# Attention slots of a one-core hybrid decoder block: query loads and splits earlier, the next head's keys and values split during its predecessor's fourth query block, reciprocals beside the first transposes

## The chip, the cores and the metric

The kernel runs on one core of one Trainium2 chip. The metric is the device time of one execution in microseconds (us); lower is better. Before the change it takes 2336.98 us as the median of three runs (2335.45 to 2340.22). The engines are called PE (matrix multiplies and transposes), ACT (activations and copies), DVE and POOL (elementwise work), and SP, which only issues the DMAs of this kernel. Each engine works through its own instructions in the order in which the program lists them; an instruction that waits holds up everything behind it on that engine.

## The reference, cut to what matters

One decoder block on 2048 positions of width 1024: a projection, eight heads of causal "forgetting" attention beside a gated linear recurrence, an output projection, and a gate with a second embedding. Only the attention is touched here. Per head of width 128, with `c` the running sum of the log forget gates:

```
s = einsum('bhqd,bhkd->bhqk', qi, k) * scale
s = s + (ci[:, :, :, None] - c[:, :, None, :])
s = where(kpos[None, :] <= qpos[:, None], s, -inf)
w = softmax(s, axis=-1)
o = einsum('bhqk,bhkd->bhqd', w, v)
```

Everything is float32. The kernel gets there with three matrix multiplies for every product: each operand is split into a rounded high part and the remainder, `hi` and `lo`, and hi·hi, hi·lo and lo·hi are added up (`mm3`).

## The kernel before, in words

The program has three parts: the projections and the recurrence, which spill queries, keys, values and gates to DRAM; the attention; and the output projections.

The attention is written as a list of **slots** that run one after the other, in an order fixed by hand. A head has 40 of them. They belong to four query blocks `g` of 512 queries: block 0 attends to 512 keys and owns slots 0 to 3, block 1 slots 4 to 11, block 2 slots 12 to 23, block 3 slots 24 to 39. A (head, block) pair is a stage, `n` in the code, and `t0[n]` is its first slot. One slot handles one piece of 128 keys (`sb`). In the order of the code, slot `t` does the following (`run_slot`, L800):

- the loads registered under `before` (SP);
- the score pieces that fall due (`score_units`, L612): three matmuls on PE from `qh`, `ql`, `kh`, `kl` into one of four score banks (`sbank`), then on DVE one custom instruction that adds the bias or the masked diagonal `dg` and keeps the running minimum `m` of the negated scores (L625, followed by a short read of `m`). These are the scores of the *next* stage: those of block `g` are spread over the slots of the block ahead of it, beginning three slots before its `t0` (LEAD). So block 1's start at slot 37 of the head before, block 2's at slot 1, block 3's at slot 9, and the next head's block 0's at slot 21;
- `add_values` (L670) for slot `t-3`: three matmuls on PE from `th`, `tl` and `vh`, `vl` into the single output bank `obank`. After a stage's last one, `finish_unit` (L686) multiplies `obank` with the spread reciprocals `rb` on DVE, which frees the bank; the next stage's first `add_values` waits for it;
- `turn_probs` (L658): PE transposes four blocks of probabilities into `tbank` (L663), ACT copies them to `th`, DVE takes the remainder `tl`;
- `spread_sums` (L678), in a stage's second slot: PE transposes the reciprocals `r4` (L682), ACT copies them to `rb`;
- on DVE the gating `gs` (L691) of a finished stage; on ACT the exponentials of complete score rows (L634), and behind the fourth of them on DVE the reciprocal of the four row sums (L638);
- what is registered under `after`: the splits. `split_u` (L509) splits the queries, the high part `qh` on ACT and the rest `ql` on DVE, and adds the causal mask to the four `dg` on POOL (L516). `split_piece` (L468) splits one of the eight pieces of the next head's keys and values, `kh`/`vh` on ACT and `kl`/`vl` on POOL. `add_squares` (L693) runs on POOL two slots after a finished stage.

Where the splits fall is set by a few numbers. For stage `n`, `s0` is the slot of its first score piece; its queries, bias and diagonals are loaded at `lo`, and split and masked at `min(lo+4, s0-1)`. That is slot 33 for the next head's block 1, slot 0 for block 2, slot 5 for block 3, slot 17 for the next head's block 0. Key and value pieces 0 to 7 of the next head are split at slots 6, 10, 14 and so on to 34, each loaded six slots earlier into one of three `kvf` buffers. The query load has one buffer, `qf`. All loads and the store of `gs` go through SP in the order of the code.

## Time and profile before

One execution was profiled. Its own time is 2336.76 us, its span 2335.0 us from the first to the last instruction.

| | us |
|---|---|
| median of three runs | 2336.98 |
| the profiled execution | 2336.76 |
| its span | 2335.0 |
| attention: first score matmul to last gating | 1138.4 to 1745.1 |
| one head in the middle (third head: slot 0's transposes to the fourth head's) | 1295.43 to 1367.02 |
| granted PE clock, mean | 0.996 |

All times below are from the start of the span. In the timeline a row has a start, a duration, the engine, the line, what is written from what, a count, and in brackets the idle time of the engine just before it with what ended it. Consecutive instructions of an engine overlap a little in the records, so the distance between two starts, not the duration, is what one costs in a queue: a `tl` of 0.69 us is followed 0.60 us later. The rows of the third head stand for all of them, since the heads repeat.

### The profile page before, as it was taken

How to read it: one execution, taken by the hardware profiler on the slowest of the kernel's cores; microseconds unless marked ns; L12 is line 12 of the kernel's file. 1: busy time of each engine (PE TensorE's matmuls, PEld its weight loads, DVE VectorE, ACT ScalarE, POOL GpSimd, SP SyncE). 2: the span in 40 equal slices, each digit the busy share in tenths (PEclk: the TensorE clock that was granted, in tenths of full speed). 3: DMA queues.
4: the chain of work that ended last, by engine and by line, in shares of the span. 5: the costliest groups of instructions: out<-in, count | busy, mean ns of one | idle time of the engine just before them, and what ended most of it. 6: DMA issues, size and time to landing. Idle time of an engine off the chain costs nothing.

```text
span 2335.0 us, 30636 instructions
## 1 busy us (share of the span) xinstructions
PE 2272.2 (97%) x11425; PEld 1890.0 (81%) x11425; DVE 1215.0 (52%) x2190; ACT 931.8 (40%) x1558; POOL 670.6 (29%) x597
## 2 busy tenths in 40 slices
PE   8999999999999999999899999999999999999999
PEld 8998888888888888888777777787878787888887
DVE  5222675454545454545577787777833213333333
ACT  7311443333333333332466666666644323221211
POOL 0220332323232323223133334343444223322221
PEclk9999999999999999999999999999999999999999
DMA  9411111111212121212444455445435435433332
GB/s 335 136 51 37 52 63 62 55 65 51 70 50 70 50 71 47 71 46 95 156 113 132 140 153 134 120 131 133 146 113 191 164 120 194 127 109 117 109 108 80
DMA packets 169012, 249.02 MB, mean 107 GB/s; under 512 B 14240, under 2 KB 87200, under 8 KB 168864
## 3 DMA queue, kind: packets, MB, share of 16 engines
q1 hardware_dynamic: 168720, 247.03, 33.9%
q8 instruction: 89, 1.46, 0.3%
q14 instruction: 59, 0.48, 0.1%
q10 hardware_dynamic: 144, 0.05, 0.0%
HBM read 171.26 MB, written 75.76 MB: 106 GB/s over the span
## 4 chain that ended last, share of the span: by engine, by line
PE 89%; ACT 3%; issue 2%; DVE 2%; DMA 2%; POOL 1%; SPq 0%; DVEq 0%; ACTq 0%; POOLq 0%
PE bank L60 23%; PE bank L62 23%; PE bank L61 23%; PE tbank L663 4%; PE obank L61 2%; PE obank L60 2%; PE obank L62 2%; PE sbank L60 2%; PE sbank L62 2%; PE sbank L61 2%; ACT pr L634 1%; DVE pr L625 1%; ACT th L46 1%; PE bank L1012 1%; DMA dg<-nb_d 1%
## 5 line engine op out<-in xcount | busy, mean ns | idle before, releaser
L60 PE MATMUL bank<-xh,wh 128*128 128x512 f32 x1280 | 506.0, 395 | 0.0
L61 PE MATMUL bank<-xl,wh 128*128 128x512 f32 x1280 | 505.9, 395 | 0.0
L62 PE MATMUL bank<-xh,wl 128*128 128x512 f32 x1280 | 505.9, 395 | 0.0
L61 PEld LDWEIGHTS bank<-xl,wh 128*128 128x128 f32 x1280 | 240.5, 188 | 58.0
L62 PEld LDWEIGHTS bank<-xh,wl 128*128 128x128 f32 x1280 | 240.5, 188 | 58.0
L60 PEld LDWEIGHTS bank<-xh,wh 128*128 128x128 f32 x1280 | 240.5, 188 | 57.9
L46 ACT ACTIVATE th<-tbank 128x512 fp32r<-128x512 f32 (+1 forms) x320 | 170.1, 532 | 177.1 <-PE tbank L663 171.7
L52 DVE TENSOR_TENSOR tl<-tbank,th 128x512 fp32r<-128x512 f32 (+1 forms) x320 | 194.7, 609 | 80.5 <-ACT th L46 76.8
L663 PE MATMUL tbank<-ident,pr 128*128 128x128 f32 x1088 | 172.2, 274 | 0.0
L52 POOL TENSOR_TENSOR wl<-wf,wh 128x512 fp32r<-128x512 f32 x70 | 96.0, 1392 | 265.1 <-ACT wh L46 265.1
L634 ACT ACTIVATE pr<-pr,m 128x128 f32<-128x128 f32 (+15 forms) x128 | 153.7, 1201 | 25.0 <-DVE m L625 23.6
L663 PEld LDWEIGHTS tbank<-ident,pr 128*128 128x128 f32 x1088 | 134.3, 141 | 29.1 <-issue 0.2
L60 PE MATMUL sbank<-kh,qh 128*128 128x512 f32 (+3 forms) x320 | 135.4, 423 | 23.1 <-ACT qh L46 19.1
L52 POOL TENSOR_TENSOR yo<-yf,yh 128x1024 fp32r<-128x1024 f32 x32 | 76.9, 2404 | 258.1 <-ACT yh L46 258.1
L60 PE MATMUL bank<-wvh,xh 128*128 128x256 f32 (+1 forms) x512 | 144.2, 285 | 6.2 <-ACT wvh L46 6.2
L62 PE MATMUL bank<-wvh,xl 128*128 128x256 f32 (+1 forms) x512 | 144.8, 284 | 0.0
L60 PE MATMUL obank<-th,vh 128*128 128x512 f32 (+1 forms) x320 | 124.3, 389 | 20.8 <-ACT th L46 14.6
L61 PE MATMUL bank<-wvl,xh 128*128 128x256 f32 (+1 forms) x512 | 144.4, 284 | 0.0
L61 PE MATMUL obank<-tl,vh 128*128 128x512 f32 (+1 forms) x320 | 117.8, 368 | 1.3 <-DVE tl L52 0.5
L62 PE MATMUL obank<-th,vl 128*128 128x512 f32 (+1 forms) x320 | 117.4, 367 | 0.0
L62 PE MATMUL sbank<-kh,ql 128*128 128x512 f32 (+3 forms) x320 | 117.3, 367 | 0.0
L61 PE MATMUL sbank<-kl,qh 128*128 128x512 f32 (+3 forms) x320 | 116.8, 365 | 0.0
(218 smaller groups left out, 4595.6 us busy)
## 6 DMA issues: line engine op xcount, KB each, us to landing
wf<-in_w_t_dram SPq DMA_DIRECT2D x80, 256.0 KB, 3.0
xr<-in_x_dram SPq DMA_DIRECT2D x16, 512.0 KB, 6.5
v_d<-vo SPq DMA_DIRECT2D x64, 128.0 KB, 2.2
kT_d<-st SPq DMA_DIRECT2D x32, 256.0 KB, 2.1
yl_d<-G SPq DMA_DIRECT2D x32, 256.0 KB, 2.1
qT_d<-st SPq DMA_DIRECT2D x32, 256.0 KB, 2.1
gT_d<-st SPq DMA_DIRECT2D x32, 256.0 KB, 2.2
dg<-nb_d SPq DMA_DIRECT2D x32, 256.0 KB, 7.3
```

Of the source, the lines that this page charges most:

```text
L46: nc.scalar.activation(hi, src, AF.Copy)
L52: eng.tensor_tensor(out=lo, in0=src, in1=f32(hi), op=ALU.subtract)
L60: nc.tensor.matmul(out, lhsT=wh, rhs=xh, start=start, stop=False)
L61: nc.tensor.matmul(out, lhsT=wh, rhs=xl, start=False, stop=False)
L62: nc.tensor.matmul(out, lhsT=wl, rhs=xh, start=False, stop=stop)
L625: nc.vector.tensor_tensor_reduce(out=pr[0][:, a:z], in0=b[:, :z - a], in1=u.dg[i][1] if z == L else u.bias[:, a:z], scale=-1.0, scalar=BIG ...
L634: nc.scalar.activation(pr[0][:, :L], pr[0][:, :L], AF.Exp, bias=m2, scale=-1.0, accum_out=u.r4[:, i:i + 1])
L663: nc.tensor.transpose(b[:, i * P:(i + 1) * P], u.P[i][:, sb * P:(sb + 1) * P], ident)
L1012: nc.tensor.transpose(b[:, k * P:(k + 1) * P], ht[:, kk * P:(kk + 1) * P], ident)
```

## The change

Four things move; no arithmetic is added or removed.

1. Query loads get two `qf` buffers and are issued four slots earlier; they are split at `lo+1`. That is slot 30 for block 1 (from 33), slot 38 for block 2 (from 0), slot 2 for block 3 (from 5), slot 14 for the next head's block 0 (from 17).
2. The masking of the diagonals stays where it was, now as `mask_u`.
3. The next head's piece 0 of keys is split at slot 16, and pieces 1 to 7 at slots 25, 27, 29, 31, 33, 35 and 37, each loaded five slots earlier, still into three buffers.
4. The reciprocal of a stage leaves the fourth exponential and stands behind the `tl` of the stage's first slot, one slot ahead of `spread_sums`, which reads it.

```diff
-    def load_u(h, g):
+    def load_uq(h, g):
         u = Ctx()
...
-            u.qf = ap.tile([P, 512], F32, name="qf", bufs=1)
+            u.qf = ap.tile([P, 512], F32, name="qf", bufs=2)
             nc.sync.dma_start(out=u.qf, in_=qT_d[h, :, g * 512:(g + 1) * 512])
+        return u
+
+    def load_u(h, g, u):
         if g > 0:
...
             split(nc, u.qf, u.qh, u.ql, "act", "dve")
+
+    def mask_u(u):
         for _, dg in u.dg:
...
                 u.P.append(pr[0])
-                if i == 3:
-                    nc.vector.reciprocal(u.r4, u.r4)
             return exponential
...
+        at(before, lo - 4, lambda n=n: do_load_q(n))
         at(before, lo, lambda n=n: do_load(n))
-        at(after, min(lo + 4, s0 - 1) if n > 1 else 0, lambda n=n: do_split(n))
+        at(after, min(lo + 1, s0 - 1) if n > 1 else 0, lambda n=n: do_split(n))
+        at(after, min(lo + 4, s0 - 1) if n > 1 else 0, lambda n=n: mask_u(units[n]))
...
-        base = t0[4 * (h - 1)] + 6
+        base = t0[4 * (h - 1)]
         for p_ in range(8):
-            at(before, base + 4 * p_ - 6, lambda h=h, p_=p_: load_piece(h, p_))
-            at(after, base + 4 * p_, lambda h=h, p_=p_: split_piece(h, p_))
+            a = base + (16 if p_ == 0 else 23 + 2 * p_)
+            at(before, a - 5, lambda h=h, p_=p_: load_piece(h, p_))
+            at(after, a, lambda h=h, p_=p_: split_piece(h, p_))
...
             turn_probs(stages[n][1], units[n], sb)
+            if sb == 0:
+                nc.vector.reciprocal(units[n].r4, units[n].r4)
             if sb == 1:
```

PE's instructions stand in the same order as before. Three places show what moves on ACT and DVE.

ACT from slot 37 to slot 1 of the following head (the exponentials write `pr` and the row sums `r`; their width tells the row). Before:

```order
L634 ACTIVATE pr,r_10545<-pr,m 128x640
L46 ACTIVATE th<-tbank 128x256
L634 ACTIVATE pr,r_10545<-pr,m 128x768
L46 ACTIVATE th<-tbank 128x128
L634 ACTIVATE pr,r_10545<-pr,m 128x896
L46 ACTIVATE th<-tbank 128x512
L634 ACTIVATE pr,r_10545<-pr,m 128x1024
L46 ACTIVATE qh<-qf 128x512
L46 ACTIVATE th<-tbank 128x384
```

The same stretch of the changed kernel:

```order
L638 ACTIVATE pr,r_10544<-pr,m 128x640
L46 ACTIVATE vh<-kvf 128x512
L46 ACTIVATE th<-tbank 128x256
L638 ACTIVATE pr,r_10544<-pr,m 128x768
L46 ACTIVATE qh<-qf 128x512
L46 ACTIVATE th<-tbank 128x128
L638 ACTIVATE pr,r_10544<-pr,m 128x896
L46 ACTIVATE th<-tbank 128x512
L638 ACTIVATE pr,r_10544<-pr,m 128x1024
L46 ACTIVATE th<-tbank 128x384
```

Block 2's query split moves from behind the exponential of width 1024 to behind that of width 768, and the last piece of values comes in ahead of it.

DVE from slot 12, the first of block 2, on (`pr,m<-sbank` are score pieces, `on` frees the output bank). Before:

```order
L52 TENSOR_TENSOR tl<-tbank,th 128x512
L625 ISA pr,m<-sbank,bias,m 128x512
L625 ISA m 128x1
L52 TENSOR_TENSOR tl<-tbank,th 128x512
L625 ISA pr,m<-sbank,dg_11575,m 128x256
L625 ISA m 128x1
L688 TENSOR_TENSOR on<-obank,rb 128x512
L52 TENSOR_TENSOR tl<-tbank,th 128x512
L691 TENSOR_TENSOR gs<-on,gs 128x512
L625 ISA pr,m<-sbank,bias 128x512
```

The changed kernel from the same `tl` on:

```order
L52 TENSOR_TENSOR tl<-tbank,th 128x512
L835 RECIPROCAL r_11580<-r_11580 128x4
L629 ISA pr,m<-sbank,bias,m 128x512
L629 ISA m 128x1
L52 TENSOR_TENSOR tl<-tbank,th 128x512
L629 ISA pr,m<-sbank,dg_11572,m 128x256
L629 ISA m 128x1
L690 TENSOR_TENSOR on<-obank,rb 128x512
L52 TENSOR_TENSOR tl<-tbank,th 128x512
L693 TENSOR_TENSOR gs<-on,gs 128x512
L52 TENSOR_TENSOR ql<-qf,qh 128x512
```

The reciprocal stands behind the first `tl` of the block, and the `ql` of the next head's block 0 now comes in slot 14, behind the gating, instead of in slot 17.

ACT from slot 21 to slot 28, around the start of block 3. Before:

```order
L46 ACTIVATE th<-tbank 128x384
L634 ACTIVATE pr,r_11179<-pr,m 128x128
L46 ACTIVATE th<-tbank 128x256
L46 ACTIVATE kh<-kvf 128x512
L46 ACTIVATE th<-tbank 128x128
L46 ACTIVATE th<-tbank 128x512 x2
L684 ACTIVATE rb<-tbank 128x512
L634 ACTIVATE pr,r_11179<-pr,m 128x256
L46 ACTIVATE th<-tbank 128x512
L46 ACTIVATE vh<-kvf 128x512
```

The changed kernel:

```order
L46 ACTIVATE th<-tbank 128x384
L638 ACTIVATE pr,r_11164<-pr,m 128x128
L46 ACTIVATE th<-tbank 128x256
L46 ACTIVATE th<-tbank 128x128
L46 ACTIVATE th<-tbank 128x512 x2
L686 ACTIVATE rb<-tbank 128x512
L638 ACTIVATE pr,r_11164<-pr,m 128x256
L46 ACTIVATE vh<-kvf 128x512
L46 ACTIVATE th<-tbank 128x512 x2
L46 ACTIVATE kh<-kvf 128x512
```

The piece at slot 22 is gone, and from slot 25 on a piece follows every second slot.

## The prediction

> **What bounds the kernel now.** I read the page first, then who PE waited for during the attention, then one head by stretches, then the single rows of each wait.

> ```profile
> PE 2272.2 (97%) x11425; PEld 1890.0 (81%) x11425; DVE 1215.0 (52%) x2190; ACT 931.8 (40%) x1558; POOL 670.6 (29%) x597
> PE 89%; ACT 3%; issue 2%; DVE 2%; DMA 2%; POOL 1%; SPq 0%; DVEq 0%; ACTq 0%; POOLq 0%
> ...
> PE sbank L60 <- ACT qh L46: 19.1, 8, 2.4
> PE obank L60 <- ACT th L46: 14.6, 15, 1.1
> PE obank L60 <- DVE on L688: 6.2, 9, 0.9
> ```

> PE is busy for 97% of the span and carries 89% of the chain that ended last. The change leaves PE's list alone, so it can only win PE's waits. The three lower rows are PE's waits from 1138 to 1760 us (who waited for whom: us in total, times, longest): 19.1 + 14.6 + 6.2 = 39.9 us. That is the most that can be won, 1.7% of the time. They repeat once per head, in four places. In the third head:

> ```profile
> 1298.41 0.50 PE L60 MATMUL sbank<-kh,qh 128*128 128x512 f32 x1 [2.39 <-ACT qh L46]
> 1311.59 0.47 PE L60 MATMUL obank<-th,vh 128*128 128x512 f32 x1 [0.59 <-DVE on L688]
> 1341.60 0.45 PE L60 MATMUL obank<-th,vh 128*128 128x384 f32 x1 [1.06 <-ACT th L46]
> 1346.49 0.47 PE L60 MATMUL obank<-th,vh 128*128 128x512 f32 x1 [0.92 <-ACT th L46]
> ```

> These are slots 1, 7, 24 and 27. The second question is whether another engine would stop PE once these waits go. Busy times by stretch of the head (slots 0-3, 4-11, 24-27, 28-35, and the whole head; columns: length, then PE, PEld, DVE, ACT, POOL):

> ```profile
> 1295.43:1305.10 9.67, 7.28 (x46) 6.09 (x45) 7.05 (x18) 5.12 (x10) 1.95 (x3) 1.00 0.51 157
> 1305.10:1321.59 16.49, 15.89 (x92) 13.43 (x91) 14.29 (x40) 11.67 (x19) 8.48 (x9) 1.00 0.62 183
> 1342.65:1348.00 5.35, 4.43 (x35) 4.00 (x34) 4.32 (x9) 3.69 (x10) 2.22 (x2) 1.00 0.21 52
> 1348.00:1358.72 10.72, 10.72 (x65) 8.99 (x64) 7.88 (x15) 7.45 (x16) 4.92 (x6) 1.00 0.46 135
> 1295.43:1367.02 71.59, 66.47 (x394) 56.27 (x393) 56.44 (x137) 48.34 (x88) 27.28 (x32) 1.00 0.45 134
> ```

> In slots 0-3, PE works 7.28 us and DVE 7.05: when PE stops waiting, DVE has next to nothing left. So the query wait will not be won whole.

> **A: block 2's queries, slots 38 to 7.** The split moves from slot 0 to slot 38, so the 2.39 us wait on `qh` goes. What is late next is DVE. Its list from the end of slot 38's `tl` to the `on` that frees the output bank in slot 6:

> ```profile
> 1292.14 0.94 ACT L634 ACTIVATE pr<-pr,m 128x768 f32<-128x768 f32 x1
> 1292.98 0.19 ACT L634 ACTIVATION_READ_ACCUMULATOR pr<-pr,m 128x1 f32 x1
> 1292.47 0.68 DVE L625 CUSTOM_DVE_ANT_0 pr<-sbank,bias 128x512 f32<-128x512 f32 x1
> 1310.76 0.69 DVE L688 TENSOR_TENSOR on<-obank,rb 128x512 f32<-128x512 f32 x1
> 1292.47:1311.45 18.98, 16.13 (x97) 13.57 (x95) 15.07 (x41) 11.95 (x23) 6.41 (x10) 1.00 0.53 171
> ...
> L46 ACT ACTIVATE qh<-qf x30: 613/618/633, 1153.3 to 1667.0; 128x512 fp32r<-128x512 f32 x30
> ...
> DVE tl L52 <- ACT th L46: 1.2, 3, 0.6
> DVE ql L52 <- ACT qh L46: 0.7, 2, 0.3
> DVE pr L625 <- PE sbank L62: 0.6, 1, 0.6
> DVE r L638 <- ACT pr L634: 0.4, 1, 0.4
> ```

> Of 18.98 us DVE works 15.07. The four listed waits are 2.9; the distances between starts that exceed an instruction's own cost add some 0.7 in short ones, so 3.6 can go. Against it stand two new stalls. In slot 38 `ql` now follows `tl`, whose successor starts at 1292.47 now and 0.1 later with the new `vh` piece ahead of `th`. `qh` waits behind the 0.94 us exponential, which then starts at about 1292.24, and the read of its row sum, which ends at 1293.17 (1292.98 + 0.19); `qh` takes 0.62 and ends at 1293.79. DVE stands from 1292.57, about 1.25. The same happens in slot 2 for block 3: by the same counting down both lists, DVE is done with `gs` at 1302.2 and `qh`, behind the exponential of width 1152, at 1302.7, another 0.48. The reciprocal of block 0 adds 0.11. So `on` ends 3.6 - 1.7 - 0.1 = 1.8 us earlier and PE resumes slot 7 by that much earlier; on the way it loses 0.4 and 0.8 us at `spread_sums` of slots 1 and 5, wanted at 1298.3 and 1305.6 while DVE's list reaches the reciprocals at 1298.5 and 1306.3, but these lie inside the DVE chain and are not counted again. The listed waits alone give 2.9 - 1.7 = 1.2; the whole of PE's two waits is 2.39 + 0.59 = 2.98. I take **1.75** per head, ends 1.0 and 2.98.

> **B: the next head's first queries, slots 14 to 24.**

> ```profile
> 1334.30 0.69 DVE L52 TENSOR_TENSOR ql<-qf,qh 128x512 fp32r<-128x512 f32 x1 [1.70 <-ACT qh L46]
> 1334.90 0.68 DVE L625 CUSTOM_DVE_ANT_0 pr<-sbank,bias 128x512 f32<-128x512 f32 x1
> 1339.07 2.01 ACT L634 ACTIVATE pr<-pr,m 128x2048 f32<-128x2048 f32 x1 [1.00 <-DVE m L625]
> 1341.20 0.18 DVE L638 RECIPROCAL r<-r 128x4 f32<-128x4 f32 x1 [1.56 <-ACT pr L634]
> 1341.08 0.47 ACT L46 ACTIVATE th<-tbank 128x384 fp32r<-128x384 f32 x1
> ```

> The 1.06 us wait at slot 24 is for this `th`, which stands behind the exponential of width 2048, which waits for the last `m`, which is late since DVE stood 1.70 for `qh` and then did `ql`, 0.60. In slot 14 `ql` stalls too, behind the exponential of width 1792, by about 1.0, so DVE starts slot 15 some 1.6 late; but with nothing to wait for in slot 17 it reaches slot 18's first score piece at 1333.4 instead of 1334.90. From there to the start of the big exponential it takes 1339.07 - 1334.90 = 4.2 now and some 0.5 more then, since the exponential of width 1920 also comes later and holds up one `th`: 1338.1 instead of 1339.07. `th` ends at 1340.5 instead of 1341.55. So 1.0 of the 1.2 us (1.06, and the remainder `tl` behind it) goes: **1.0** per head, for the seven heads that have a successor; ends 0 and 1.2.

> **C: the reciprocals.** They leave DVE's path, which frees the 1.56 us above, but `spread_sums` now follows `tl` of the stage's first slot. Rows of blocks 2 and 3:

> ```profile
> 1322.95 0.69 DVE L52 TENSOR_TENSOR tl<-tbank,th 128x512 fp32r<-128x512 f32 x1 [0.61 <-ACT th L46]
> 1323.52 0.60 PE L682 MATMUL tbank<-ident,r 128*128 128x128 f32 x4
> 1343.92 0.69 DVE L52 TENSOR_TENSOR tl<-tbank,th 128x512 fp32r<-128x512 f32 x1 [0.49 <-ACT th L46]
> 1344.23 0.60 PE L682 MATMUL tbank<-ident,r 128*128 128x128 f32 x4
> ```

> The reciprocal starts 0.60 behind `tl`'s start and takes 0.18: done at 1323.73 and 1344.70. PE's transposes of it started at 1323.52 and 1344.23, so with some 0.1 for the handover they come 0.3 and 0.5 to 0.6 late. Behind them on PE stand the scores, the values and the next transposes. In block 3 the delay falls into the 0.92 us wait of slot 27, which hangs on `on` and not on these, and costs nothing; if that cover went it would cost 0.5. In block 2 nothing covers it: **-0.3** per head, ends 0 and -0.5.

> **D: the pieces.** Seven of eight now fall in slots 25 to 37. In slots 24 to 35 there were three, and six will be there: three more at 0.62 on ACT and 1.30 on POOL. ACT's 3.69 + 7.45 = 11.1 of 15.15 us that PE works becomes 13.0, POOL's 7.1 becomes 11.0. Neither is full, and a `th` has three slots, some 3.4 us, until it is used. Cost 0, hidden beside PE's values and transposes. The cover ends if a piece lands late (rival 3). On SP the loads of queries move ahead of diagonals and waits for free `kvf` buffers move behind; `qf` needs 3.9 us to land (row under rival 3) and has five slots.

> [...]

> ```profile
> 1311.95 0.68 DVE L691 TENSOR_TENSOR gs<-on,gs 128x512 f32<-128x512 f32 x1
> 1347.08 1.31 POOL L52 TENSOR_TENSOR vl<-kvf,vh 128x512 fp32r<-128x512 f32 x1 [2.76 <-ACT vh L46]
> 1347.13 1.81 DVE L691 TENSOR_TENSOR gs<-on,gs 128x512 f32<-128x512 f32 x1
> ```

> `gs` takes 0.68 alone, and 1.81 where POOL's `vl` began 0.05 us earlier: 1.13 more. [...]

> **Sum.** 8 x 1.75 + 7 x 1.0 - 8 x 0.3 = 14.0 + 7.0 - 2.4 = 18.6 us. From the profiled execution, 2336.76, that gives **2318.2**; the median of the runs is 0.22 higher, so nothing is corrected.

> **The rivals.**

> 1. *DVE takes nothing back.* If its short gaps absorb the two new stalls, PE wins 2.98 in A and 1.2 in B: 8 x 2.98 + 7 x 1.2 - 2.4 = 29.8, giving 2307. Against it: 7.05 of 7.28 us in slots 0-3.
> [...]
> 3. *Pieces land late: slower.* With three buffers, piece 4's load waits until POOL is done with piece 1, in the middle of slot 27, and piece 6's until it is done with piece 3. Median us from issue to landing, and all `kvf` loads' least, median and longest:

> ```profile
> kvf<-kT_d SPq DMA_DIRECT2D x28, 256.0 KB, 4.3
> kvf<-v_d SPq DMA_DIRECT2D x28, 256.0 KB, 3.3
> qf<-qT_d SPq DMA_DIRECT2D x30, 256.0 KB, 3.9
> ...
> DMA to landing us min/median/max: 2.6/3.5/9.1
> ```

> Piece 4, issued about 1348.9, lands at 4.3 just when ACT reaches it, about 1353; the `th` behind it has some 2 us to spare. So it decides at a landing of 6.3 us. At the longest one seen, 9.1, pieces 4 and 6 would cost 2.8 each: 2 x 2.8 x 7 = 39 us less the gain of 18.6, giving 2357. Against it: the median.
> 4. *Nothing.* The queries are split earlier but ACT and DVE are the pace everywhere, and PE waits at other places for the same time: 2336. Against it: DVE's 56.44 of 71.59 us per head.

> **How the numbers follow.** Forecast (2312 to 2325) 0.55; rival 1 0.15; rival 2 0.15; rival 4 0.07; rival 3 0.08. About 0.2%, 4.7 us, is what a measurement can tell from no change: faster is below 2332.3, slower above 2341.7. Faster: 0.55 + 0.15 and most of rival 2, 0.14: 0.84. Same: 0.01 + 0.07 = 0.08. Slower: 0.08. The range runs from rival 1's end, less 2, to 2332: 2305 to 2332.

> **What would show it.** PE's `qh` wait gone, its slot-24 wait near 0.2, slot 27's still there in part; new PE waits at the transposes of `r` in slots 1, 5, 13 and 25; DVE standing for `qh` about 1.2 us in slot 38 and 1.0 in slot 14; one head in about 69.2 us, from 71.6. I am wrong if ACT waits for `kvf` long enough that `th` makes PE wait in slots 32 to 39, or if `ql` grows from 0.69 to 1.8 in slot 38.

## Result, and the profile after

| | before | after |
|---|---|---|
| median, us (lowest to highest, 6 runs each) | 2337.21 (2335.45 to 2340.99) | 2351.16 (2349.26 to 2354.34) |
| span of the profiled execution, us | 2335.0 | 2348.8 |
| granted PE clock, mean | 0.996 | 0.995 |

The changed kernel is **slower** by 14 us: ratio 1.0058, 95% interval 1.0045 to 1.0071. That is 33 us from the forecast and outside the range.

The page of the changed kernel, PE's row and the chain that ended last:

```profile
PE 2285.0 (97%) x11425; PEld 1889.8 (80%) x11425; DVE 1204.9 (51%) x2190; ACT 927.1 (39%) x1558; POOL 670.9 (29%) x597
PE 84%; DMA 4%; DVE 4%; ACT 3%; issue 2%; POOL 1%; SPq 1%; DVEq 0%; ACTq 0%; POOLq 0%
```

PE carries 84% of the chain instead of 89%, and transfers 4% instead of 2%. PE also has 12.8 us more busy time with the same 11425 instructions. Slower matmuls are the smaller part of that: by the clock records the time at half clock (0.50) grew from 17.1 to 24.8 us. In that time 128x512 matmuls start 0.43 us apart, at full clock 0.23 us (medians from 1138 us on, both kernels); the 7.7 us more are worth 3.9 us of work at most. Slots 4 to 6 of seven heads show 2.6 us more busy time at a clock of 1.00 throughout: short hold-ups count as busy, such as a score matmul that starts 0.43 us behind its predecessor instead of 0.23. The attention's waits say where to look. First who PE waits for in the changed kernel, from 1138 to 1775 us (us in total, times, longest), then ACT's waits for transfers in the same stretch:

```profile
PE sbank L60 <- DVE m L629: 24.7, 14, 3.6
PE tbank L684 <- DVE r L835: 15.1, 23, 1.0
PE obank L60 <- ACT pr L638: 2.9, 7, 0.4
...
PE obank L60 <- ACT th L46: 0.8, 1, 0.8
PE obank L60 <- DVE on L690: 0.5, 1, 0.5
```

```profile
ACT kh L46 <- DMA kvf<-kT_d: 28.8, 7, 5.6
...
ACT qh L46 <- DMA qf<-qT_d: 1.9, 1, 1.9
```

The three waits that made up the 39.9 us of before are nearly gone: `qh` 19.1 to none in PE's list, `th` 14.6 to 0.8 (slot 27's part is left with 2.9, now listed under `pr`), `on` 6.2 to 0.5. Two stand in their place: the reciprocals, 15.1, and one of 24.7 (3.0 before), in which the score banks wait for `m`. ACT's row points at what is behind the greater part of that one: seven times, once per head that has a successor, ACT stands for a piece of keys.

The second head by stretches, changed kernel (slots 0-3, 4-11, 12-23, 24-35, 36-39; columns as in the prediction), and then the last stretch, slots 36-39, of before:

```profile
1229.59:1237.55 7.96, 7.19 (x46) 6.04 (x44) 7.47 (x20) 6.17 (x12) 1.83 (x2) 1.00 0.45 152
1237.55:1254.48 16.93, 16.36 (x92) 13.32 (x90) 15.42 (x42) 10.62 (x16) 4.22 (x6) 1.00 0.49 154
1254.48:1274.75 20.27, 20.05 (x116) 16.58 (x115) 15.91 (x40) 13.97 (x25) 5.26 (x7) 1.00 0.31 89
1274.75:1290.87 16.12, 15.34 (x98) 12.95 (x97) 11.09 (x23) 11.94 (x25) 8.33 (x8) 1.00 0.38 107
1290.87:1304.32 13.45, 10.13 (x48) 8.24 (x47) 5.64 (x15) 5.07 (x12) 6.83 (x9) 0.87 0.57 176
```

```profile
1287.13:1295.43 8.30, 8.30 (x48) 7.17 (x47) 7.02 (x21) 5.39 (x12) 2.29 (x4) 1.00 0.65 197
```

Slots 36 to 39 take 13.45 us where they took 8.30: 5.15 more. Of these PE stands still for 13.45 - 10.13 = 3.32, and is 10.13 - 8.30 = 1.83 longer busy with the same 48 instructions (matmuls and transposes), at a granted clock of 0.87. The stretches ahead of slot 36 took 9.68, 16.83, 21.08 and 16.07 us in the same head of before: none is longer by more than 0.1.

The chain runs backwards from PE's one long stop there. The rows of PE, DVE, ACT and of SP's own queue, changed kernel:

```profile
1298.67 0.50 PE L60 MATMUL sbank<-kh,qh 128*128 128x512 f32 x1 [3.32 <-DVE m L629]
```

```profile
1297.45 0.69 DVE L52 TENSOR_TENSOR tl<-tbank,th 128x512 fp32r<-128x512 f32 x1 [5.69 <-ACT th L46]
1298.06 0.55 DVE L629 CUSTOM_DVE_ANT_0 pr<-sbank,bias 128x384 f32<-128x384 f32 x1
```

```profile
1296.31 0.63 ACT L46 ACTIVATE kh<-kvf 128x512 fp32r<-128x512 f32 x1 [5.28 <-DMA kvf<-kT_d]
1296.84 0.96 ACT L46 ACTIVATE th<-tbank 128x512 fp32r<-128x512 f32 x2
```

```profile
1280.53 0.32 SPq L463 DMA_DIRECT2D kvf<-kT_d  x1
1282.64 0.32 SPq L465 DMA_DIRECT2D kvf<-v_d  x1
1283.01 0.42 SPq L710 DMA_DIRECT2D ya_d<-gs  x1
1283.49 0.42 SPq L502 DMA_DIRECT2D bias<-nb_d  x1
1283.95 1.95 SPq L508 DMA_DIRECT2D dg<-nb_d  x4
1286.26 0.32 SPq L463 DMA_DIRECT2D kvf<-kT_d  x1
1287.99 0.59 SPq L465 DMA_DIRECT2D kvf<-v_d  x1
```

PE waits for a score bank, since DVE has not read the scores in it. DVE has not, since a `tl` stands ahead on its queue, and that waits for ACT's `th`. The `th` stands behind `kh` on ACT's queue, and `kh` waits 5.28 us for **piece 6** of the keys, the load issued at 1286.26. Right ahead of it on SP stand the next head's block 1: its bias and four broadcast loads of diagonals. From issue to landing, for pieces 4, 5, 6 and 7 in this order (least, median and longest of the one load):

```profile
DMA to landing us min/median/max: 2.8/2.8/2.8
DMA to landing us min/median/max: 3.1/3.1/3.1
DMA to landing us min/median/max: 10.0/10.0/10.0
DMA to landing us min/median/max: 8.9/8.9/8.9
```

Pieces of the same size land in 2.8 and 3.1 us ahead of the broadcast loads and in 10.0 and 8.9 behind them. Over the seven heads piece 6 takes 7.0 to 10.3 us, pieces 4 and 5 take 2.8 to 3.8. PE's stop between slots 38 and 39 lasts 0.3 to 3.6 us, 15.1 in the seven heads.

Summed over the seven heads, from one slot's first transpose on PE to the next slot's, after less before: slots 0-3 -1.8 us, 4-6 +1.8, 12-22 +1.6, 23 -7.6, 24-26 +0.5, 36-39 **+21.95**, the others 0; together +16.4. The rest of the 13.8 us between the spans lies outside these heads: +1.3 ahead of them, -0.2 in the last head, -3.6 behind.

### The profile page after: what moved, and what is told of

It is laid out like the page before. It is cut to its first block, busy times and chain, and to the rows that moved or that the text cites. A ratio compares the mean times of both kernels' runs of the same rounds, so it can differ in the third digit from the quotient of the medians.

```text
span 2348.8 us, 30663 instructions
## 1 busy us (share of the span) xinstructions
PE 2285.0 (97%) x11425; PEld 1889.8 (80%) x11425; DVE 1204.9 (51%) x2190; ACT 927.1 (39%) x1558; POOL 670.9 (29%) x597
## 4 chain that ended last, share of the span: by engine, by line
PE 84%; DMA 4%; DVE 4%; ACT 3%; issue 2%; POOL 1%; SPq 1%; DVEq 0%; ACTq 0%; POOLq 0%
PE bank L60 23%; PE bank L62 23%; PE bank L61 23%; PE tbank L665 3%; DMA dg<-nb_d 2%; DVE pr L629 2%; PE sbank L60 2%; PE obank L61 2%; PE obank L60 2%; PE sbank L61 2%; PE sbank L62 2%; PE obank L62 2%; ACT th L46 1%; PE tbank L684 1%; DMA kvf<-kT_d 1%
## 5 line engine op out<-in xcount | busy, mean ns | idle before, releaser
L60 PE MATMUL bank<-xh,wh 128*128 128x512 f32 x1280 | 506.0, 395 | 0.0
L62 PE MATMUL bank<-xh,wl 128*128 128x512 f32 x1280 | 505.9, 395 | 0.0
L62 PEld LDWEIGHTS bank<-xh,wl 128*128 128x128 f32 x1280 | 240.5, 188 | 57.9
L60 PEld LDWEIGHTS bank<-xh,wh 128*128 128x128 f32 x1280 | 240.5, 188 | 57.8
L52 DVE TENSOR_TENSOR tl<-tbank,th 128x512 fp32r<-128x512 f32 (+1 forms) x320 | 192.9, 608 | 126.1 <-ACT th L46 121.3
L46 ACT ACTIVATE th<-tbank 128x512 fp32r<-128x512 f32 (+1 forms) x320 | 167.3, 528 | 130.3 <-PE tbank L665 128.1
L638 ACT ACTIVATE pr<-pr,m 128x128 f32<-128x128 f32 (+15 forms) x128 | 153.9, 1202 | 56.5 <-DVE m L629 56.1
L52 POOL TENSOR_TENSOR wl<-wf,wh 128x512 fp32r<-128x512 f32 x70 | 96.0, 1393 | 265.1 <-ACT wh L46 265.1
L60 PE MATMUL sbank<-kh,qh 128*128 128x512 f32 (+3 forms) x320 | 138.4, 432 | 25.9 <-DVE m L629 24.7
L60 PE MATMUL bank<-wvh,xh 128*128 128x256 f32 (+1 forms) x512 | 144.1, 285 | 7.5 <-ACT wvh L46 7.5
L52 POOL TENSOR_TENSOR yo<-yf,yh 128x1024 fp32r<-128x1024 f32 x32 | 77.1, 2409 | 255.5 <-ACT yh L46 255.5
L62 PE MATMUL bank<-wvh,xl 128*128 128x256 f32 (+1 forms) x512 | 144.4, 284 | 0.0
L60 PE MATMUL obank<-th,vh 128*128 128x512 f32 (+1 forms) x320 | 125.6, 392 | 4.2 <-ACT pr L638 2.9
L62 PE MATMUL obank<-th,vl 128*128 128x512 f32 (+1 forms) x320 | 118.1, 369 | 0.0
L62 PE MATMUL sbank<-kh,ql 128*128 128x512 f32 (+3 forms) x320 | 118.0, 369 | 0.0
## 6 DMA issues: line engine op xcount, KB each, us to landing
wf<-in_w_t_dram SPq DMA_DIRECT2D x80, 256.0 KB, 3.0
kT_d<-st SPq DMA_DIRECT2D x32, 256.0 KB, 2.1
yl_d<-G SPq DMA_DIRECT2D x32, 256.0 KB, 2.1
qT_d<-st SPq DMA_DIRECT2D x32, 256.0 KB, 2.1
gT_d<-st SPq DMA_DIRECT2D x32, 256.0 KB, 2.1
dg<-nb_d SPq DMA_DIRECT2D x32, 256.0 KB, 7.4
```

Of the source, the lines that this page charges most:

```text
L46: nc.scalar.activation(hi, src, AF.Copy)
L52: eng.tensor_tensor(out=lo, in0=src, in1=f32(hi), op=ALU.subtract)
L60: nc.tensor.matmul(out, lhsT=wh, rhs=xh, start=start, stop=False)
L62: nc.tensor.matmul(out, lhsT=wl, rhs=xh, start=False, stop=stop)
L638: nc.scalar.activation(pr[0][:, :L], pr[0][:, :L], AF.Exp, bias=m2, scale=-1.0, accum_out=u.r4[:, i:i + 1])
```

## Experiments

What each had to tell apart: do the pieces alone cost the time (and are the other parts worth what was forecast), or do the other parts cost it; and if the pieces, is it the piece's place behind the broadcast loads, or its place beside other work?

**1. The change without the pieces** (`pieces_back`): the loop of the pieces as before, all else as changed.

```diff
-        base = t0[4 * (h - 1)]
+        base = t0[4 * (h - 1)] + 6
...
-            a = base + (16 if p_ == 0 else 23 + 2 * p_)
-            at(before, a - 5, lambda h=h, p_=p_: load_piece(h, p_))
-            at(after, a, lambda h=h, p_=p_: split_piece(h, p_))
+            at(before, base + 4 * p_ - 6, lambda h=h, p_=p_: load_piece(h, p_))
+            at(after, base + 4 * p_, lambda h=h, p_=p_: split_piece(h, p_))
```

> The changed kernel with the key and value pieces put back to slots 6, 10 to 34; queries and reciprocals as changed. Theory 1, a late piece: the changed kernel loses its time because ACT stands 28.8 us in all for the keys of piece 6 (slot 35), whose load is issued behind four broadcast loads of diagonals; PE then stops in slot 38, and slots 36 to 39 are 22 us longer over seven heads. Without the crowded pieces that goes and the gains in slots 7 and 24 stay: 2316 to 2326. Theory 2, DVE's pace: the queries split in slot 38 hold DVE up and PE stops for that: 2343 to 2351.

Measured: 2320.11 us (2318.09 to 2323.61), ratio 0.9930 (0.9914 to 0.9946). The second head's slots 36-39 of this kernel, and the whole head:

```profile
1285.21:1293.51 8.30, 8.30 (x48) 7.18 (x46) 5.80 (x16) 4.39 (x10) 4.25 (x7) 1.00 0.62 216
1224.14:1293.51 69.37, 67.26 (x394) 56.14 (x392) 56.68 (x137) 48.28 (x88) 26.56 (x31) 1.00 0.44 140
```

Slots 36-39 are back at 8.30 and the head is at 69.4. Queries and reciprocals bring 15.9 us, most of what was forecast for the whole change; the pieces lose it, and 30 to 31 us in all (by the ratios and by the medians).

**2. The pieces alone** (`pieces_only`): the kernel before with the changed loop of the pieces (the diff of experiment 1 read from + to -).

> The kernel before with only the pieces moved to slots 16 and 25 to 37. Theory 1: the late piece costs here too, on top of the old waits, less the room that the missing piece in slot 22 gives: 2348 to 2362, with ACT standing some 25 us for kvf. Theory 2: without the query split in slot 38 nothing is lost: 2333 to 2340.

Measured: 2377.95 us (2377.37 to 2381.24), ratio 1.0181 (1.0163 to 1.0199): the same place, but dearer than expected. ACT waits 31.5 us for `kvf` in seven heads, and slots 36-39 grow by 29.9, slots 0-3 by 9.1. The part that the expectation missed is the clock: 55.4 us of this execution ran at half clock, against 17.1 in the kernel before, which is up to 19 us (experiment 8).

**3. The queries alone** (`queries_only`): the kernel before with the two `qf` buffers, `load_uq` and `mask_u`, pieces and reciprocals as before.

```diff
+        at(before, lo - 4, lambda n=n: do_load_q(n))
         at(before, lo, lambda n=n: do_load(n))
-        at(after, min(lo + 4, s0 - 1) if n > 1 else 0, lambda n=n: do_split(n))
+        at(after, min(lo + 1, s0 - 1) if n > 1 else 0, lambda n=n: do_split(n))
+        at(after, min(lo + 4, s0 - 1) if n > 1 else 0, lambda n=n: mask_u(units[n]))
```

> The kernel before with only the query loads and splits moved. Theory 1: the query wait of slot 1 goes and DVE gives a part of it back: 2318 to 2328; the waits of slots 24 and 7 tell how much of the rest the reciprocals are worth. Theory 2: 2337 to 2346, with PE stopped for score banks in slots 38 to 1.

Measured: 2323.66 us (2322.02 to 2325.47), ratio 0.9944 (0.9929 to 0.9959). So most of the gain, 12 of the 16 us of experiment 1, comes from the queries. Slots 0-6 give 3.4 us over seven heads, slot 23 gives 7.5. PE now waits for `on` (16.1 us): the pace there is DVE's.

**4. The broadcast loads ahead of the late pieces** (`diag_early`): the changed kernel, but block 1's queries, bias and diagonals are loaded at slot 22, the queries three and the others seven slots earlier. The pieces stay.

```diff
-        at(before, lo - 4, lambda n=n: do_load_q(n))
-        at(before, lo, lambda n=n: do_load(n))
+        early = 7 if stages[n][1] == 1 and n > 1 else 0
+        at(before, lo - max(4, early), lambda n=n: do_load_q(n))
+        at(before, lo - early, lambda n=n: do_load(n))
```

> The changed kernel with one thing moved: block 1's query, bias and diagonal loads are issued at slot 22 instead of 25 and 29, so that the loads of pieces 4 to 7 no longer stand behind them. Theory 1, a late landing: ACT's wait for kvf goes from 28.8 us to under 5 and the time falls by 18 to 26 us: 2325 to 2333. Theory 3, the pieces themselves crowd ACT, POOL or the three buffers: ACT's wait shrinks little or PE stops elsewhere, 2343 to 2351. Theory 2 (DVE's pace): no change either.

Measured: 2322.22 us (2321.39 to 2324.37), ratio 0.9939 (0.9924 to 0.9954), 3 us better than the range expected. Piece 6 lands in 2.8 to 3.0 us and ACT waits 1.5 us for `kvf` instead of 28.8; slots 36-39 are as before. With the pieces exactly where the change puts them, the loss is gone, so it isn't their work on ACT and POOL. Pieces 2 and 3, now behind the broadcast loads, take 7.5 to 9.8 us, but nobody needs them so soon.

**5. One piece ahead of the broadcast loads** (`piece6_first`): the changed kernel with block 1's bias and diagonals loaded two slots later, between pieces 6 and 7.

```diff
+        late = 2 if stages[n][1] == 1 and n > 1 else 0
-        at(before, lo, lambda n=n: do_load(n))
+        at(before, lo + late, lambda n=n: do_load(n))
```

> The changed kernel with block 1's bias and diagonal loads moved two slots back, from 29 to 31, so that piece 6's load stands ahead of them and piece 7's behind them. If the order behind the broadcast loads is what makes a piece late, piece 6 lands in 3 to 4 us instead of 7 to 10, ACT no longer waits for it, and piece 7 takes 7 to 10 us and is waited for instead (vh for the values, 2 to 4 us a head): 2328 to 2348 us in all. If it is the number of bytes in that stretch, piece 6 still takes over 6 us.

Measured: 2348.89 us in a single run (before beside it 2337.95), 1 us above the range expected. SP's queue in this kernel, and ACT's wait:

```profile
1283.90 0.32 SPq L463 DMA_DIRECT2D kvf<-kT_d  x1
1284.27 0.43 SPq L502 DMA_DIRECT2D bias<-nb_d  x1
1284.74 1.85 SPq L508 DMA_DIRECT2D dg<-nb_d  x4
1286.68 0.38 SPq L465 DMA_DIRECT2D kvf<-v_d  x1
```

```profile
1296.07 0.63 ACT L46 ACTIVATE vh<-kvf 128x512 fp32r<-128x512 f32 x1 [3.45 <-DMA kvf<-v_d]
```

Piece 6, now ahead, lands in 3.0 us here (3.0 to 3.7 over the heads); piece 7, now behind, in 9.4 (8.0 to 10.4), and ACT waits for it instead. Slots 36-39 are as before, and slots 0-3 are 12.0 us longer: PE now stops between slots 0 and 1, 2.2 to 4.0 us per head for a score bank (before: 2.39 for `qh`), and five heads have a window at half clock, 1.7 us each at most (3.41 us at 0.50), that the kernel before doesn't have. So the late landing and the stop went with the place behind the broadcast loads.

**6. The reciprocals alone** (`recip_only`): the kernel before with the two edits of the reciprocal.

```diff
-                if i == 3:
-                    nc.vector.reciprocal(u.r4, u.r4)
...
+            if sb == 0:
+                nc.vector.reciprocal(units[n].r4, units[n].r4)
```

> The kernel before with only the reciprocals moved behind the first tl. The stalls of DVE for the last exponential go (1.56 us in slot 21), but the wait of slot 24 hangs on the big exponential and stays; new waits of some 0.3 us at slot 13 and at slots 1, 5, 25 where not covered: 2334 to 2342. If the stalls set the pace, 2325 to 2333.

Measured: 2348.68 us (2345.93 to 2349.79), ratio 1.0038 (1.0025 to 1.0052): a miss, 7 us above the upper end. The waits at `spread_sums` account for 2.1 us (slots 12-26). Another 5.6 us lie in slots 0-3 of the fourth to the seventh head (the eighth adds 1.6), where PE waits for `qh` as long as in the kernel before (2.39 us each), but is granted a lower clock behind it: 0.80 over the first 8.65 us of these heads, where the kernel before has 1.00.

**7. The reciprocals one slot ahead** (`recip_mid_only`): the kernel before with the reciprocal in the slot ahead of its stage's first one, so that no transpose needs to wait for it.

```diff
-                if i == 3:
-                    nc.vector.reciprocal(u.r4, u.r4)
...
+    at(after, t0[0] - 1, lambda: nc.vector.reciprocal(units[0].r4, units[0].r4))
...
+        at(after, t0[n] - 1, lambda n=n: nc.vector.reciprocal(units[n].r4, units[n].r4))
```

> The kernel before with only the reciprocals moved, but to one slot ahead of their stage's first slot, so that TensorE need not wait for them at the first transpose. If the loss of recip_only (10.7 us) comes from the waits that its place adds at spread_sums and from the granted clock that falls after them, this kernel adds no such wait and no fall: 2333 to 2339 us. If taking the reciprocal out of its old place behind the exponentials sets the loss off by itself, wherever it goes: 2343 to 2350 us, with windows of half clock in slots 0 to 3 again.

Measured: 2339.95 us (2333.18 to 2342.31, ten runs), ratio 0.9998 (0.9988 to 1.0007): no change, a little above the first expectation and below the second. So taking the reciprocal from its old place costs nothing by itself. But its second head had a window at half clock (0.50 from 1228.37 to 1231.78) that the kernel before doesn't have, with no wait added ahead of it (2.39 us for `qh` in both), so "new waits make the clock fall" doesn't hold in this form either.

**8. When the clock falls** (read from the eleven profiled kernels of this study). In the records of the kernel before and of the changed one the granted clock is 1.00 or 0.50, and all its changes lie on a grid of 3.413 us, to within 0.002 us. PE's first wait of a head is 2.39 us in the kernel before and in `recip_only` alike, but falls differently on this grid. Windows of that grid, the one with the wait and the next, for the fourth head of the kernel before, then the fifth and the sixth of `recip_only`:

```profile
1365.54:1368.95 3.41, 2.05 (x12) 1.59 (x10) 2.46 (x8) 2.47 (x5) 0.91 (x2) 1.00 0.40 155
1368.95:1372.36 3.41, 2.38 (x14) 1.91 (x15) 1.90 (x6) 0.97 (x3) 0.00 (x0) 1.00 0.23 26
```

```profile
1441.87:1445.28 3.41, 1.20 (x9) 0.89 (x7) 1.81 (x6) 2.49 (x6) 0.91 (x2) 1.00 0.27 101
1445.28:1448.69 3.41, 3.23 (x10) 2.90 (x11) 1.97 (x5) 0.13 (x1) 0.00 (x0) 0.50 0.44 105
1516.96:1520.37 3.41, 1.69 (x7) 1.22 (x8) 1.90 (x4) 1.67 (x4) 0.45 (x1) 1.00 0.08 11
1520.37:1523.78 3.41, 3.41 (x20) 3.41 (x18) 1.97 (x8) 1.09 (x2) 0.00 (x0) 0.50 0.92 263
```

In the kernel before the wait is cut in two by the grid: PE is busy for 2.05 and 2.38 of 3.41 us, and the clock stays at 1.00. In `recip_only` most of it falls into one window, with 1.20 or 1.69 us busy, and the next window runs at 0.50. Counted over all windows of the attention (1138 to 1775 us) in the eleven profiled kernels, those which ran at full clock themselves, with PE's busy time taken without overlaps:

| PE busy in a window | windows | followed by half clock |
|---|---|---|
| under 43% | 45 | 45 |
| 43 to 52% | 20 | 7 |
| over 52% | 1916 | 0 |

So a stop of 2.39 us was enough where most of it fell into one window. This is a reading of the records: no run shifted the grid on purpose. It accounts for `recip_only`, whose heads come to lie at another place on the grid (a head of 71.6 us is 20.98 windows, so successive heads fall nearly alike), and for the surplus of `pieces_only`, ten of whose windows between slot 38 of the first head and the start of the eighth ran at half clock, where the kernel before had none. In the changed kernel three heads had one. Here is the second head's:

```profile
1296.59:1300.00 3.41, 1.33 (x6) 1.08 (x7) 2.30 (x7) 1.82 (x4) 1.27 (x1) 1.00 0.70 256
1300.00:1303.41 3.41, 3.41 (x11) 2.62 (x10) 1.54 (x6) 2.81 (x8) 2.50 (x5) 0.50 0.07 24
```

Up to 1.7 of the 1.83 us of longer busy time in slots 36-39 above are this window (3.41 us at 0.50).

**9. and 10. Two versions that might beat both** (`best1`, `best2`). `best1` has the queries as changed, the pieces as before and the reciprocal of experiment 7; `best2` has the pieces as changed with the loads of experiment 4, and the same reciprocal. Against the changed kernel, both have this edit, and `best1` the diff of experiment 1, `best2` that of experiment 4:

```diff
+    at(after, t0[0] - 1, lambda: nc.vector.reciprocal(units[0].r4, units[0].r4))
...
+        at(after, t0[n] - 1, lambda n=n: nc.vector.reciprocal(units[n].r4, units[n].r4))
...
-            if sb == 0:
-                nc.vector.reciprocal(units[n].r4, units[n].r4)
```

> Queries as changed, pieces back at slots 6 to 34, and the reciprocal one slot ahead of its stage's first slot (behind the exponentials, before the first tl). If PE's waits at the transposes of the reciprocals (13.2 us in all with the pieces back) cost time by themselves, 2310 to 2316. If DVE is the pace there and PE only waits at another place, 2317 to 2323.

> The changed kernel with both repairs: block 1's loads at slot 22 and the reciprocal one slot ahead of its stage's first slot; pieces where the change put them. By the same two readings 2312 to 2318 or 2319 to 2325; it stays 0 to 3 us above the kernel with the pieces back if the crowded pieces bring nothing.

Measured: `best1` 2317.84 us (2314.96 to 2320.19), ratio 0.9905 (0.9888 to 0.9923); `best2` 2320.81 (2317.58 to 2322.16), ratio 0.9918 (0.9904 to 0.9933). Both beat the kernel before, both as the second reading has it (DVE is the pace), and the two can't be told apart by their intervals. PE's waits in `best1`:

```profile
PE obank L60 <- DVE on L690: 11.6, 16, 0.8
PE obank L60 <- ACT th L46: 7.2, 8, 0.9
```

The waits for `r` that cost 13.2 us in `pieces_back` are gone, but 11.6 + 7.2 us for `on` and `th` stand there instead, and the head is 69.0 us instead of 69.4. Seven of the eight waits listed under `th` are slot 27's, which hangs on `on` too (see C below), so what bounds these places in this trace is DVE's pace.

## Why the prediction was wrong

- **A, block 2's queries: right in kind, a little too high.** The wait for `qh` went, and DVE took a part back. In `pieces_back` slots 0-6 take 15.5 to 15.6 us from the second head on, instead of 16.9 to 17.3: about 1.5 per head where 1.75 was forecast (the waits of slots 1 and 5 within both). The first head, which begins behind the projections, loses 0.9 there, where the forecast counted it like the others. The stalls came where they were named: in the third head of `pieces_back` DVE stands for `qh` 1.17 us in slot 38 (forecast 1.25) and 0.41 in slot 2 (0.48), and PE for `r` 0.52 and 0.57 in slots 1 and 5 (0.4 and 0.8).
- **B, the next head's queries: right.** Slot 24's wait, 1.06 in the third head, falls away: 7.55 us in seven heads, 1.08 each, where 1.0 was forecast. DVE stands 1.00 for `qh` in slot 14, as reckoned.
- **C, the reciprocals: right in size.** In `pieces_back` slots 12-22 grow by 1.66 us in seven heads, 0.24 each, where 0.3 was forecast, and slots 24-26 by 0.5 in all: slot 27's wait covered the rest of slot 25's delay, as reckoned. That wait hangs on `on`, as the prediction says, though its row names `th`: the `th` of slot 24 that it needs was done by 1343.9, while `on` ends at 1346.34, 0.15 ahead of the matmul at 1346.49. Kernel before:

```profile
1345.66 0.68 DVE L688 TENSOR_TENSOR on<-obank,rb 128x512 f32<-128x512 f32 x1
```

  What the prediction had not priced is what such shifts can do to the clock (experiments 6 and 8); in the changed kernel and in `pieces_back` that did not come up at this place.
- **The sum of A to C came out close, in part by luck:** 2318.2 forecast, 2320.1 measured without the pieces. By the profiles `pieces_back` is 16.7 us shorter than the kernel before. The eight heads give 14.2 of these, not 18.6: A brought 9.8 of its 14.0, B 7.6 of 7.0, C cost 2.2 of 2.4, and the rest of the eighth head 0.9. Another 3.3 lie behind the last slot's transposes, where nothing moved, and 0.8 were lost ahead of the heads. Of the two, only the kernel before has a window of lowered clock there. From the last slot's transposes to the end, the kernel before and `pieces_back`, then that window:

```profile
1738.18:2335.00 596.82, 588.50 (x2615) 476.58 (x2613) 198.35 (x294) 152.39 (x276) 154.39 (x109) 1.00 0.41 132
1724.82:2318.30 593.48, 586.93 (x2615) 476.08 (x2613) 197.07 (x294) 152.32 (x276) 154.27 (x109) 1.00 0.41 133
1973.06:1976.47 3.41, 3.41 (x9) 2.64 (x9) 1.71 (x3) 0.90 (x2) 1.28 (x1) 0.51 0.78 237
```
- **D, the pieces: wrong, and this is the step that failed.** It read "Cost 0, hidden beside PE's values and transposes", with a cover that "ends if a piece lands late". It does: piece 6 lands after 7.0 to 10.3 us, and slots 36-39 pay 21.95 us: 15.1 of PE standing still and three windows at half clock, 1.7 each at most, for the greater part. Another 9.4 us go in slots 0-3, which gain 1.8 us in all instead of the 11.2 of `pieces_back`: 5.6 of it in the fourth to the sixth head, where PE waits 1.0 to 1.3 us for the score banks again between slots 0 and 1, and 2.1 in the first, beside two windows at half clock that `pieces_back` doesn't have.
- **Rival 3 was the mechanism, with the wrong instant and the wrong chance.** It looked for the lateness in the buffers (piece 6's load waits until POOL is done with piece 3) and set against it the median landing of 4.3 us. A buffer held piece 6's load itself for 0.3 us: it was issued at 1286.26, ahead of its need by nearly five us, and in `diag_early`, where the loss is gone, it goes out at the same distance from the head's start (56.6 us, 56.7 in the changed kernel). The buffers did set when the diagonals went out. SP stood 13.8 us at piece 4's load until POOL was done with piece 1, and block 1's bias and diagonals stand behind that load on SP (SP's waits in the second head, in all, times, longest):

```profile
SPq L463 <- POOL vl L52: 14.1, 2, 13.8
```

  What made the load land late was what stood right ahead of it on SP. The median was of two kinds of loads, and the trace of before shows both, in the seven heads: pieces 0 and 1, issued behind a block's diagonals, land in 6.2 to 9.1 us, and pieces 5 and 7, which are not, in 2.9 to 3.2. Two rows of the kernel before, the load of piece 0 at 1289.7 and of piece 7 at 1272.7:

```profile
DMA to landing us min/median/max: 6.9/6.9/6.9
DMA to landing us min/median/max: 3.1/3.1/3.1
```

  There the slow ones had the time; the change put a piece with little time into that place. With a landing of 9 us for piece 6 alone, rival 3's own bound of 6.3 would have been passed in every head. It also named piece 4, which landed in 2.8 us and cost nothing, so its price of 39 us was too high: 30 to 31 us is what the pieces cost (experiment 1).
- **Rival 2 (chance 0.15): no run shows its term.** The sign named for `ql` of slot 38, from 0.69 to 1.8, came up in small: starting at 1303.13, it takes 0.86 beside POOL's masking of the diagonals (0.79 to 0.87 in the seven heads). In `pieces_back` it is back at 0.69. In slot 30 of six heads of the changed kernel, beside a `vl` that began some 0.75 us earlier, it takes 1.08 to 1.12. In slot 2 `ql` takes 1.27 in the changed kernel and 1.26 in `pieces_back`, so that is not the pieces' doing.
- **Of "what would show it"** the sign against the forecast came up word for word: ACT waiting for `kvf` until PE stops in slots 38 to 39. The head is 72.0 to 77.4 us instead of the 69.2 forecast.

## What to carry to other kernels

Before a load is moved, write down what will stand ahead of it on its queue, and take its landing from loads that stood behind the same things: a median over loads in different places hides how far they lie apart, here from about 3 to 9 us. The late transfer cost here not the piece that it brought but everything queued behind the first instruction that waited for it: ACT stood 5.28 us at `kh` with a `th` behind it, DVE 5.69 at the `tl` that needs the `th`, PE 3.32 at the scores behind the `tl`. And look at where a stop of the matmul engine falls: one of 2.39 us was followed by no lower clock in the second to the eighth head of the kernel before, where the grid cut it in two, but in five heads of `recip_only`, where most of it fell into one window of 3.41 us, by a window at 0.50, worth up to 1.7 us.
